# Weight tiles of 128x1024 in rings of three in place of 128x512 in rings of five, and shared places for tiles of the solve and of the samples

## The chip, the cores and the metric

The kernel runs on one core of a Trainium2 chip. The metric is the device time of one execution in microseconds; the kernel before has a median of 2118.79 us in three runs. TensorE is called PE in the profile, VectorE DVE, ScalarE ACT, GpSimd POOL, and SyncE, which issues the DMAs here, SP.

## The reference

One inference step of two layers for a prompt of 272 rows (16 meta tokens and 256 tokens) and 8 samples of one token each; the model width is 2048 and the branch width 4096. All data are fp32.

```python
# layer 0 (mixer A, RWKV-7), for prompt and samples
rkvz = einsum('btpd,pde->btpe', xm[:, :, :4], w_rkvz)        # 4 products 2048 x 4096
...                                                          # decay d, a from two low-rank products; kk normalised per head
S = S * d - (S @ kk) * b + v * k ; y = S @ r                 # 64 heads, state 64 x 64, row after row
y = groupnorm(y) + (r*k*r_k).sum() * v ; o = (y * silu(z)) @ w_out     # 4096 x 2048
# shared keys and values
kv = rmsnorm(h, kv_norm) @ w_kv                              # 2048 x 1024
# layer 1 (mixer B): sliding window of 128, a sink per head, 64 query heads on 8 kv heads
q, z = split(rmsnorm(h, b_norm) @ b_w_qz)                    # 2048 x 8192
h += (attention(q, k, v, sinks) * silu(z)) @ b_w_o           # 4096 x 2048
```

The outputs are the final rows, the RWKV states, the shift rows and the caches of prompt and samples.

## The kernel before

**Weights.** Every weight matrix is read once, in units of 256 KB (`wunits`, L199): 128 partitions by 512 numbers, which are two k-tiles of 256 columns. A unit goes through three engines. SP issues its DMA into `raw` (L211). ACT casts it to `whi`, a rounded fp32r copy (L195, in `split`). DVE subtracts, `wlo = raw - whi` (L197, in `split`). PE then makes three matmuls for each k-tile and half of the columns (`mm3`, L218 to L220: whi by xh, whi by xl, wlo by xh), 12 for a unit, each with 280 moving rows (272 + 8) in layer 0 and 264 in layer 1. There are 1040 such units: 112 named k, 128 each named v, r, z, oa, qb, zb and ob, and 32 named kv. `raw`, `whi` and `wlo` are rings of five tiles each; from the products of out_a on (where `self.wx` is set) every second unit takes its raw tile from another ring of four, `rawx`. A raw tile comes free with its subtract, `whi` and `wlo` with the last matmul that reads them.

**Stages by time.** Phase 0 (to about 155 us) normalises and mixes the inputs. Phase A (to about 1260 us) runs the products r, k, v, z and the first part of the output product, and between their pieces, on the same engines, the recurrence: the preparation of a pair of heads (`prep`), scores, `substitute` and `solve` (a triangular inverse by blocks), `chain` (40 steps of three matmul groups each, with copies on ACT and DVE between), `group_norm` and the samples' `decode`. Then come out_a (to 1376 us), the kv product (to about 1415 us), phase B (attention and the products q and z, to 1912 us) and out_b, with a tail to the end.

**What sets the order.** On PE the order is the program's: `drive` takes a piece of a product (one unit, half of its columns, 6 matmuls) and then whatever a stream has due at that place, so the matmuls of the recurrence stand at fixed places between weight pieces. An engine executes in order, so a small matmul whose operand is late holds the weight matmuls behind it. On DVE, ACT and SP a scheduler sets the order by priority and by `issue_after`; the streams other than the epilogues and the main one are issued after the subtract `self.los[-2]`. `self.raws` and `self.los` hold one entry for each unit, and code elsewhere indexes them by unit.

**Places the change and the prediction touch.** `substitute` (L1053) ends with two transposes on DVE, TN (L1081) and TR (L1082), which `solve` multiplies first (L1102, ps_so). `prep` (L858) loads kT (a ring of two tiles), multiplies it into kk (L898, which waits for a DMA of the key norms that `key_norms` writes), and scans the decays (L910, cl). `group_norm` transposes the result on PE (L1275, ps_yt) and adds it on DVE (L1276, vT), which frees the bank. `decode` multiplies the samples' states into a work tile T, tag dT. In the kv product (from L1490) the casts stand on ACT between operations of `norm_mix` (L1464, bmh).

Of the kernel before, what the change touches and what calls it, by code (L numbers as in the profile page):

```python
# [12 lines left out]
F32 = mybir.dt.float32  # L13
# [96 lines left out]
class Kernel:  # L110
# [10 lines left out]
    def run(self):  # L121
        nc, tc = self.nc, self.tc
        with contextlib.ExitStack() as st:
            pool = lambda n, bufs=1, **k: st.enter_context(tc.tile_pool(name=n, bufs=bufs, **k))
            self.cp = pool("const")
            self.wp = pool("wts", 5)
            self.pm = pool("pm", 3, space=PSUM)
            self.pp = pool("pp", 1, space=PSUM)
            self.pe = pool("pe", 2, space=PSUM)
            self.dp = pool("dram", space=DRAM)  # L130
            self.single_banks()
            self.load_consts()
            self.sp = self.open("stage", bufs=2)
            self.mp = self.open("mix", bufs=8, side="right")
            self.ph = self.open("ph0")
            self.phase0()
            self.close("ph0")
            tile = dict(reuse_waits="tile")

            pools = self.open("late", **tile), self.open("early", **tile)  # L140
            self.rp = Pools(pools, "vT Y ev gmean gvar rsyy rsty")
            self.close("py", "pc")
            self.pcy = self.open("pcy", 1, space=PSUM)
            self.phase_a()
            self.close("pcy")
            self.single_banks()
            self.close("mix")
            right = dict(side="right", **tile)
            self.op = self.open("res", **right)
            self.kvp, self.st0, self.wx0 = (self.open(n, **right) for n in ("kv", "st0", "wx0"))  # L150
            self.out_a()
            self.close("gA", "late", "stage")
            self.bp = self.open("B", **tile)
            self.phase_b()
            self.close("B")
            self.gp = self.open("gB", **tile)
            self.out_b()
            self.wx = None
            self.close("gB", "g1", "st1", "wx1", "g0", "at", "res", "py", "pc")
# [39 lines left out]
    def wunits(self, w, name, nk, col, nc_, per):  # L199

        nc = self.nc
        assert nc_ == 256 and per == 2, (nc_, per)
        for k0 in range(0, nk, per):
            t = lambda n, dt, **k: self.wp.tile([128, 512], dt, tag=n, name=f"{n}_{name}_{col}_{k0}", **k)[
                :, :per * nc_].rearrange("p (k c) -> p k c", k=per)
            if self.wx and len(self.raws) % 2:
                raw = self.wx.tile([128, 512], F32, tag="rawx", bufs=4, name=f"raw_{name}_{col}_{k0}")[
                    :, :per * nc_].rearrange("p (k c) -> p k c", k=per)
            else:
                raw = t("raw", F32, bufs=5)  # L210
            self.raws.append(nc.sync.dma_start(raw.rearrange("p k c -> p (k c)"), w[col // 256, k0 // 2]))  # L211
            hi, lo = t("whi", F32R), t("wlo", F32R)
            self.los.append(self.split(hi, lo, raw))
            yield k0, hi, lo

    def mm3(self, ps, wh, wl, xh, xl, start, stop):
        mm = self.nc.tensor.matmul
# [640 lines left out]
    def prep(self, u):  # L858
        nc, rp, I = self.nc, self.rp, self.I
# [6 lines left out]
        w = lambda n, bufs=1: rp.tile([128, 2, N], F32, tag=n, bufs=bufs, name=f"{n}{u}")  # L866

        raw = rp.tile([LR, 512], F32, tag="lraw", name=f"lraw_{u}")
# [3 lines left out]
        hi = rp.tile([128, 544], F32R, tag="lhi", name=f"lhi_{u}")[:LR, :512]  # L872
        lo = rp.tile([128, 544], F32R, tag="llo", name=f"llo_{u}")[:LR, :512]
# [11 lines left out]
        cl, a = wa  # L885
        if u >= 4:
            yield 0, self.after(6, ('n', u // 4), *(('x', m, p0) for m in range(3)))
        else:
            yield 0, self.after(6, ('x', 0, p0))
        kT = w("kT", 2)  # L890
        dma(kT, self.kd[b][:, sl])
        rT = w("rT")
        dma(rT, self.rd[b][:, sl])
# [44 lines left out]
        g, h0 = p0 // 8, (2 * p0) % 16  # L938
# [114 lines left out]
    def substitute(self, o):  # L1053

        nc, rp = self.nc, self.rp
# [3 lines left out]
        w = lambda n, *s: rp.tile([128, *s], F32, tag=n, name=f"{n}{o}")  # L1059
# [8 lines left out]
        NL = w("NL", 512)  # L1068
        V.transpose(NL, N16.rearrange("p i t -> p t i"))
        nl = NL.rearrange("p (t a s) -> p t a s", a=2, s=16)  # L1070
        for s in range(1, 15):
            n = 15 - s
# [4 lines left out]
            V.tensor_tensor(nl[:, s + 1:16, :, 0:s], nl[:, s + 1:16, :, 0:s], tv, op=AD)  # L1077
        for a in range(2):
            V.memset(NL[:, 16 * a:512:33], 1.0)
        TN, TR = w("TN", 16, 32), w("TR", 16, 32)  # L1080
        V.transpose(TN.rearrange("p s i -> p (s i)"), nl.rearrange("p t a s -> p s a t"))  # L1081
        V.transpose(TR.rearrange("p t i -> p (t i)"), NL)  # L1082
        TT = rp.tile([128, 20, 64], F32, tag="TT", name=f"TT{o}")
# [198 lines left out]
    def decode(self, g):  # L1282
# [18 lines left out]
        NI = 8  # L1301
        rowb = lambda a: a.unsqueeze(1).to_broadcast((128, NI, 64))
        for q in range(64 // NI):
            if q:
                yield 3
            S = rp.tile([128, NI, 64], F32, tag="dS", bufs=1, name=f"dS{g}_{q}")
            T = rp.tile([128, NI, 64], F32, tag="dT", bufs=1, name=f"dT{g}_{q}")
            iq = slice(NI * q, NI * q + NI)
            dma(S.rearrange("p i j -> p (i j)"),
                I['state_wkv'][g, q])  # L1310
            yield 5 if g < 3 else 4, lambda: self.samples
            for w, o in ((kk, sa), (dr, y)):
                tt(T, S, rowb(w), op=MU)
                V.reduce_sum(o[:, iq], T, axis=AX.X)
# [658 lines left out]
```

## Time and profile before

| | |
|---|---|
| three runs | 2116.79, 2118.79 and 2124.86 us, median 2118.79 |
| profiled execution | 2118.32 us, its span 2116.5 us |
| granted PE clock | 0.99 in the mean |
| DMA | 446.28 MB, mean 211 GB/s |
| DVE instructions counted as busy | 4112, 1697.8 us |
| ACT instructions counted as busy | 2790, 1263.8 us |

The span is the stretch from the first to the last recorded event; the profiled execution's time is 1.8 us longer. A row of the waits gives an engine, what it was about to do, what it waited for, the sum of these waits in us, their number and the longest. In rows of the timeline the columns are start, duration, engine, line, operation, tiles (out<-in), and in brackets the idle time before it with its releaser; the lines that the prediction shows are not shown here.

### The profile page before, as it was taken

The page shows a single profiled execution, that of the slowest core. Times are in us where ns is not written, and L with a number is a line of the kernel's source. Part 1 is how long each engine was busy: PE and PEld are TensorE (multiplying, and loading weights), DVE is VectorE, ACT ScalarE, POOL GpSimd, SP SyncE. Part 2 cuts the span into 40 slices and gives each one's busy share as a digit, 9 for nine tenths or more (in the row PEclk, how much of TensorE's full clock was granted, in tenths as well). Part 3 has the DMA queues.
Part 4 walks back from the last instruction along what each step waited for, and adds up shares of the span by engine and source line. Part 5 has one row for each costly group of instructions (what it writes and reads, how often), then busy time and mean ns, then how long its engine had stood idle before and what let it go on. Part 6 is the DMA issues. An engine that isn't in the chain of part 4 may idle for free.

```text
span 2116.5 us, 55871 instructions
## 1 busy us (share of the span) xinstructions
PE 2064.9 (98%) x21420; PEld 1965.8 (93%) x21420; DVE 1697.8 (80%) x4112; ACT 1263.8 (60%) x2790; POOL 122.5 (6%) x188
## 2 busy tenths in 40 slices
PE   9999999899999999999999999999999999999997
PEld 7999899889899989899999999999999999999997
DVE  8867777687678878888888788997888888878885
ACT  3457766576766757767676445565565655544443
POOL 0011100001010010100100001100000000000000
PEclk9999999999999999999999999999999999999999
DMA  7898667658756876777657687757455444567774
GB/s 258 314 312 250 189 213 241 188 181 290 216 180 205 260 229 198 211 217 222 203 152 246 207 257 243 247 172 227 132 167 156 146 155 130 181 210 247 232 219 132
DMA packets 276356, 446.28 MB, mean 211 GB/s; under 512 B 54056, under 2 KB 97768, under 8 KB 275696
## 3 DMA queue, kind: packets, MB, share of 16 engines
q1 hardware_dynamic: 275656, 441.66, 66.6%
q8 instruction: 168, 2.75, 0.5%
q10 hardware_dynamic: 432, 1.05, 0.1%
q14 instruction: 100, 0.82, 0.1%
HBM read 381.69 MB, written 65.03 MB: 211 GB/s over the span
## 4 chain that ended last, share of the span: by engine, by line
PE 87%; DVE 5%; ACT 3%; DMA 3%; issue 2%; SPq 0%; POOL 0%; DVEq 0%; POOLq 0%; ACTq 0%
PE ps_z L218 6%; PE ps_z L219 6%; PE ps_z L220 6%; PE ps_k L218 3%; PE ps_ob L218 3%; PE ps_ob L220 3%; PE ps_v L218 3%; PE ps_ob L219 3%; PE ps_r L218 3%; PE ps_q L218 3%; PE ps_q L220 3%; PE ps_q L219 3%; PE ps_k L219 3%; PE ps_k L220 3%; PE ps_v L220 3%; PE ps_v L219 3%
## 5 line engine op out<-in xcount | busy, mean ns | idle before, releaser
L218 PE MATMUL ps_z<-mhlm,whi_z 128*128 128x280 f32 x512 | 158.6, 310 | 2.8 <-ACT sr L937 2.0
L219 PE MATMUL ps_z<-mhlm,whi_z 128*128 128x280 f32 x512 | 150.6, 294 | 0.0
L220 PE MATMUL ps_z<-mhlm,wlo_z 128*128 128x280 f32 x512 | 150.3, 294 | 0.0
L218 PE MATMUL ps_q<-bmh,whi_qb 128*128 128x264 f32 x512 | 150.0, 293 | 0.1
L218 PE MATMUL ps_z<-bmh,whi_zb 128*128 128x264 f32 x512 | 147.4, 288 | 0.0
L220 PE MATMUL ps_q<-bmh,wlo_qb 128*128 128x264 f32 x512 | 145.6, 284 | 0.6 <-DVE wlo_qb L197 0.6
L219 PE MATMUL ps_q<-bml,whi_qb 128*128 128x264 f32 x512 | 145.6, 284 | 0.0
L219 PE MATMUL ps_z<-bml,whi_zb 128*128 128x264 f32 x512 | 145.5, 284 | 0.0
L220 PE MATMUL ps_z<-bmh,wlo_zb 128*128 128x264 f32 x512 | 145.4, 284 | 0.0
L218 PE MATMUL ps_ob<-ghi,whi_ob 128*128 128x264 f32 x512 | 145.3, 285 | 0.0
L220 PE MATMUL ps_ob<-ghi,wlo_ob 128*128 128x264 f32 x512 | 144.6, 284 | 0.0
L219 PE MATMUL ps_ob<-glo,whi_ob 128*128 128x264 f32 x512 | 144.6, 283 | 0.0
L195 ACT CAST whi_ob<-raw_ob 128x512 fp32r<-128x512 f32 x128 | 79.1, 620 | 96.9 <-PE ps_ob L219 77.8
L195 ACT CAST whi_oa<-raw_oa 128x512 fp32r<-128x512 f32 x128 | 79.2, 620 | 88.0 <-PE ps_oa L219 30.6
L197 DVE TENSOR_TENSOR wlo_r<-raw_r,whi_r 128x512 fp32r<-128x512 f32 x128 | 87.8, 691 | 42.6 <-ACT whi_r L195 41.3
L218 PE MATMUL ps_v<-mhlm,whi_v 128*128 128x280 f32 x384 | 119.8, 312 | 0.4 <-ACT st L790 0.4
L218 PE MATMUL ps_k<-mhlm,whi_k 128*128 128x280 f32 x384 | 119.1, 310 | 1.0 <-ACT st L790 1.0
L195 ACT CAST whi_v<-raw_v 128x512 fp32r<-128x512 f32 x128 | 79.0, 619 | 65.8 <-PE ps_v L219 37.7
L197 DVE TENSOR_TENSOR wlo_v<-raw_v,whi_v 128x512 fp32r<-128x512 f32 x128 | 87.3, 687 | 36.9 <-ACT whi_v L195 35.6
L195 ACT CAST whi_zb<-raw_zb 128x512 fp32r<-128x512 f32 x128 | 78.2, 619 | 62.9 <-PE ps_z L219 38.5
L220 PE MATMUL ps_k<-mhlm,wlo_k 128*128 128x280 f32 x384 | 112.4, 293 | 2.1 <-issue 2.1
L219 PE MATMUL ps_v<-mhlm,whi_v 128*128 128x280 f32 x384 | 112.7, 293 | 0.0
(478 smaller groups left out, 7604.1 us busy)
## 6 DMA issues: line engine op xcount, KB each, us to landing
raw_k<-a_w_rkvz SPq DMA_DIRECT2D x128, 256.0 KB
raw_v<-a_w_rkvz SPq DMA_DIRECT2D x128, 256.0 KB
raw_r<-a_w_rkvz SPq DMA_DIRECT2D x128, 256.0 KB
raw_z<-a_w_rkvz SPq DMA_DIRECT2D x128, 256.0 KB
raw_oa<-a_w_out SPq DMA_DIRECT2D x128, 256.0 KB
raw_qb<-b_w_qz SPq DMA_DIRECT2D x128, 256.0 KB
raw_zb<-b_w_qz SPq DMA_DIRECT2D x128, 256.0 KB
raw_ob<-b_w_o SPq DMA_DIRECT2D x128, 256.0 KB
```

The source lines that it names most:

```text
L195: self.nc.scalar.copy(hi, src)
L197: return self.nc.vector.tensor_tensor(lo, src, hi.bitcast(F32), op=ALU.subtract)
L218: mm(ps, wh, xh, start=start, stop=False)
L219: mm(ps, wh, xl, start=False, stop=False)
L220: return mm(ps, wl, xh, start=False, stop=stop)
```

## The change

`wunits` makes tiles of 128x1024 that hold two consecutive units. One DMA of 512 KB loads both (two runs of 2 KB for each partition), one cast makes both halves of `whi`, one subtract both of `wlo`; `self.raws` and `self.los` get the same entry twice. The three rings have three such tiles, so six units where there were five. From out_a on, every fourth pair takes its raw tile from `rawx`, which has one tile of 128x1024 where it had four of 128x512. The matmuls read halves of the tiles and stay as they are, 12 for a unit.

To make room, three tiles change places: kT has one tile where it had two (so its load for a pair of heads waits for the last reader of the pair before), TN takes a place in the ring `ev` of two, and T of `decode` takes the place of NL, the tile of `substitute`.

```diff
--- before.py
+++ after.py
@@ -123,7 +123,7 @@
         with contextlib.ExitStack() as st:
             pool = lambda n, bufs=1, **k: st.enter_context(tc.tile_pool(name=n, bufs=bufs, **k))
             self.cp = pool("const")
-            self.wp = pool("wts", 5)
+            self.wp = pool("wts", 3)
             self.pm = pool("pm", 3, space=PSUM)
             self.pp = pool("pp", 1, space=PSUM)
             self.pe = pool("pe", 2, space=PSUM)
@@ -199,19 +199,20 @@
     def wunits(self, w, name, nk, col, nc_, per):
 
         nc = self.nc
-        assert nc_ == 256 and per == 2, (nc_, per)
-        for k0 in range(0, nk, per):
-            t = lambda n, dt, **k: self.wp.tile([128, 512], dt, tag=n, name=f"{n}_{name}_{col}_{k0}", **k)[
-                :, :per * nc_].rearrange("p (k c) -> p k c", k=per)
-            if self.wx and len(self.raws) % 2:
-                raw = self.wx.tile([128, 512], F32, tag="rawx", bufs=4, name=f"raw_{name}_{col}_{k0}")[
-                    :, :per * nc_].rearrange("p (k c) -> p k c", k=per)
+        assert nc_ == 256 and per == 2 and nk % 4 == 0, (nc_, per, nk)
+        for k0 in range(0, nk, 4):
+            nm = f"{name}_{col}_{k0}"
+            t = lambda n, dt: self.wp.tile([128, 1024], dt, tag=n, name=f"{n}_{nm}")
+            if self.wx and len(self.raws) // 2 % 4 == 1:
+                raw = self.wx.tile([128, 1024], F32, tag="rawx", bufs=1, name=f"raw_{nm}")
             else:
-                raw = t("raw", F32, bufs=5)
-            self.raws.append(nc.sync.dma_start(raw.rearrange("p k c -> p (k c)"), w[col // 256, k0 // 2]))
+                raw = t("raw", F32)
+            self.raws += [nc.sync.dma_start(raw.rearrange("p (u c) -> p u c", u=2),
+                                            w[col // 256, k0 // 2:k0 // 2 + 2].rearrange("u p c -> p u c"))] * 2
             hi, lo = t("whi", F32R), t("wlo", F32R)
-            self.los.append(self.split(hi, lo, raw))
-            yield k0, hi, lo
+            self.los += [self.split(hi, lo, raw)] * 2
+            for u in range(2):
+                yield k0 + 2 * u, *(a[:, 512 * u:512 * u + 512].rearrange("p (k c) -> p k c", k=per) for a in (hi, lo))
 
     def mm3(self, ps, wh, wl, xh, xl, start, stop):
         mm = self.nc.tensor.matmul
@@ -887,7 +888,7 @@
             yield 0, self.after(6, ('n', u // 4), *(('x', m, p0) for m in range(3)))
         else:
             yield 0, self.after(6, ('x', 0, p0))
-        kT = w("kT", 2)
+        kT = w("kT")
         dma(kT, self.kd[b][:, sl])
         rT = w("rT")
         dma(rT, self.rd[b][:, sl])
@@ -1077,7 +1078,7 @@
             V.tensor_tensor(nl[:, s + 1:16, :, 0:s], nl[:, s + 1:16, :, 0:s], tv, op=AD)
         for a in range(2):
             V.memset(NL[:, 16 * a:512:33], 1.0)
-        TN, TR = w("TN", 16, 32), w("TR", 16, 32)
+        TN, TR = ev("TN", 16, 32), w("TR", 16, 32)
         V.transpose(TN.rearrange("p s i -> p (s i)"), nl.rearrange("p t a s -> p s a t"))
         V.transpose(TR.rearrange("p t i -> p (t i)"), NL)
         TT = rp.tile([128, 20, 64], F32, tag="TT", name=f"TT{o}")
@@ -1304,7 +1305,7 @@
             if q:
                 yield 3
             S = rp.tile([128, NI, 64], F32, tag="dS", bufs=1, name=f"dS{g}_{q}")
-            T = rp.tile([128, NI, 64], F32, tag="dT", bufs=1, name=f"dT{g}_{q}")
+            T = rp.tile([128, 512], F32, tag="NL", name=f"dT{g}_{q}").rearrange("p (i j) -> p i j", i=NI)
             iq = slice(NI * q, NI * q + NI)
             dma(S.rearrange("p i j -> p (i j)"),
                 I['state_wkv'][g, q])
```

Line numbers after `wunits` are higher by one in the changed kernel. Over the whole program the busy instructions on DVE fall by 520, those on ACT by 520, and SP's DMA issues from 1785 to 1265.

The first place is on DVE, ahead of the first solve (about 252 to 256 us): the end of `substitute`, with TN, for which PE waits in ps_so. kk and cl belong to the preparation of a later pair of heads, wlo_r is a weight subtract. Before:

```order
L197 TENSOR_TENSOR wlo_r_10_3533<-raw_r_10_3530,whi_r_10_3532 128x512
L898 SCALAR_TENSOR_TENSOR kk_3641<-kT_3637,par,kk_3641 128x280 x2
L1075 TENSOR_TENSOR stmp_14_3002<-NL_2961 128x28
L910 SCALAR_TENSOR_TENSOR cl_3338<-reset,cl_3338 128x272 x2
L1077 TENSOR_TENSOR NL_2961<-NL_2961,stmp_14_3002 128x2x14
L1081 STREAM_TRANSPOSE TN_3007<-NL_2961 128x512
L1082 STREAM_TRANSPOSE TR_3008<-NL_2961 128x512
```

Now:

```order
L1078 TENSOR_TENSOR NL_2685<-NL_2685,stmp_13_2723 128x4x13
L1076 TENSOR_TENSOR stmp_14_2726<-NL_2685 128x28
L1078 TENSOR_TENSOR NL_2685<-NL_2685,stmp_14_2726 128x2x14
L1082 STREAM_TRANSPOSE TN_2731<-NL_2685 128x512
L1083 STREAM_TRANSPOSE TR_2732<-NL_2685 128x512
L1105 COPY ET_3171<-ps_so_3106 128x256
L197 TENSOR_TENSOR wlo_r_12_3298<-raw_r_12_3295,whi_r_12_3297 128x1024
L899 SCALAR_TENSOR_TENSOR kk_3311<-kT_3307,par,kk_3311 128x280 x2
L911 SCALAR_TENSOR_TENSOR cl_3026<-reset,cl_3026 128x272 x2
```

The products kk and the scans cl, which stood between the last steps of NL and TN, now stand behind TN, TR, the copy ET and a weight subtract.

The second place is on DVE in the product v, at the second solve and the first group norm (about 371 to 382 us); ps_yt is PE's bank of the group norm, which vT frees. kk is the row that waits for the DMA of the key norms. Before:

```order
L898 SCALAR_TENSOR_TENSOR kk_5449<-kT_5445,par,kk_5449 128x280
L1075 TENSOR_TENSOR stmp_14_5118<-NL_5077 128x28
L898 SCALAR_TENSOR_TENSOR kk_5449<-kT_5445,par,kk_5449 128x280
L910 SCALAR_TENSOR_TENSOR cl_4871<-reset,cl_4871 128x272 x2
L904 TENSOR_TENSOR kT_5445<-kT_5445,km_4_5454 128x280
L1077 TENSOR_TENSOR NL_5077<-NL_5077,stmp_14_5118 128x2x14
L197 TENSOR_TENSOR wlo_v_14_5425<-raw_v_14_5422,whi_v_14_5424 128x512
L904 TENSOR_TENSOR kT_5445<-kT_5445,km_4_5457 128x280
L906 TENSOR_TENSOR ta_4872<-ta_4872,kk_5449 128x560
L1081 STREAM_TRANSPOSE TN_5123<-NL_5077 128x512
L1082 STREAM_TRANSPOSE TR_5124<-NL_5077 128x512
L1276 SCALAR_TENSOR_TENSOR vT_2043<-ps_yt_0_5399,par,vT_2043 128x272
```

Now:

```order
L1076 TENSOR_TENSOR stmp_14_4674<-NL_4633 128x28
L1078 TENSOR_TENSOR NL_4633<-NL_4633,stmp_14_4674 128x2x14
L1082 STREAM_TRANSPOSE TN_4679<-NL_4633 128x512
L1083 STREAM_TRANSPOSE TR_4680<-NL_4633 128x512
L197 TENSOR_TENSOR wlo_v_12_4933<-raw_v_12_4930,whi_v_12_4932 128x1024
L911 SCALAR_TENSOR_TENSOR cl_4445<-reset,cl_4445 128x272 x2
L899 SCALAR_TENSOR_TENSOR kk_4969<-kT_4965,par,kk_4969 128x280 x2
L1277 SCALAR_TENSOR_TENSOR vT_1857<-ps_yt_0_4925,par,vT_1857 128x272
L905 TENSOR_TENSOR kT_4965<-kT_4965,km_4_4974 128x280
```

TN, TR and the weight subtract now stand ahead of kk, so do the scans cl, and the products kT stand behind vT; between kk and vT no other row is left.

## The prediction

> **What bounds the kernel now.** I read the page first, then the stretches of 200 us, the waits of PE, ACT and SP, and last the timeline around the longest waits. The page:
>
> ```profile
> span 2116.5 us, 55871 instructions
> PE 2064.9 (98%) x21420; PEld 1965.8 (93%) x21420; DVE 1697.8 (80%) x4112; ACT 1263.8 (60%) x2790; POOL 122.5 (6%) x188
> PE 87%; DVE 5%; ACT 3%; DMA 3%; issue 2%; SPq 0%; POOL 0%; DVEq 0%; POOLq 0%; ACTq 0%
> ```
>
> PE is busy for 98% of the span. It stands for 2116.5 - 2064.9 = 51.6 us, and the change leaves all of its matmuls as they are. So the time can fall by the part of the 51.6 us that DVE and ACT cause, and by what follows such waits; it can rise without a bound of that kind. The stretches show where PE stands (columns: span, busy us and count of PE, PEld, DVE, ACT, POOL, granted clock, DMA share, GB/s):
>
> ```profile
> 200.00:400.00 200.00, 188.22 (x2357) 176.44 (x2356) 144.32 (x331) 130.23 (x287) 18.69 (x28) 0.97 0.67 211
> 600.00:800.00 200.00, 195.41 (x2578) 183.34 (x2578) 162.52 (x358) 130.48 (x282) 18.09 (x28) 0.98 0.71 223
> 1600.00:1800.00 200.00, 200.00 (x1719) 192.40 (x1717) 167.52 (x632) 116.05 (x320) 0.00 (x0) 1.00 0.49 147
> 1800.00:2000.00 200.00, 200.00 (x1657) 199.26 (x1656) 166.00 (x309) 100.90 (x177) 5.30 (x6) 1.00 0.70 217
> ```
>
> In phase B and out_b PE never stands, though DVE is 84% busy there; in phase A it loses 11.8 us in one stretch and 4.6 in another. The waits of PE say for whom:
>
> ```profile
> PE ps_yt L1275 <- DVE vT L1276: 8.0, 2, 6.9
> PE ps_so L1102 <- DVE TN L1081: 6.1, 2, 3.5
> PE ps_z L218 <- ACT sr L937: 2.0, 1, 2.0
> PE ps_kv L218 <- ACT whi_kv L195: 1.8, 1, 1.8
> PE ps_ch L1205 <- ACT W L1196: 1.3, 2, 0.9
> PE ps_ch L1191 <- DVE X L1227: 1.1, 1, 1.1
> PE ps_ch L1214 <- ACT X L1210: 1.1, 2, 0.9
> PE ps_q L220 <- DVE wlo_qb L197: 0.6, 2, 0.4
> ```
>
> Weights are waited for in two rows only, 1.8 + 0.6 = 2.4 us in 1040 units. The large waits are for the recurrence: 14.1 us in the first two rows. The stream of weights is ahead, as the waits of ACT and of SP's queue show:
>
> ```profile
> ACT whi_ob L195 <- PE ps_ob L219: 77.8, 55, 1.9
> ```
> ```profile
> SPq L211 <- DVE wlo_zb L197: 110.0, 85, 8.3
> ```
>
> The cast waits for PE to free a place, the DMA for a subtract to free one. A faster cast or transfer by itself therefore buys nothing. What can matter is where a cast or a subtract stands ahead of an operand of the recurrence.
>
> A wait costs more than its length. Behind the 6.9 us wait, in two adjoining stretches:
>
> ```profile
> 383.00:388.00 5.00, 5.00 (x27) 4.99 (x26) 1.66 (x5) 2.82 (x5) 0.00 (x0) 0.58 0.66 210
> 388.00:398.00 10.00, 10.00 (x316) 9.57 (x315) 6.49 (x14) 4.98 (x13) 0.32 (x1) 1.00 0.66 196
> ```
> ```profile
> 386.16 0.43 PE L218 MATMUL ps_v<-mhlm,whi_v 128*128 128x280 f32 x1
> 386.40 0.43 PE L219 MATMUL ps_v<-mhlm,whi_v 128*128 128x280 f32 x1
> ...
> 388.12 0.29 PE L218 MATMUL ps_v<-mhlm,whi_v 128*128 128x280 f32 x1
> 388.25 0.29 PE L219 MATMUL ps_v<-mhlm,whi_v 128*128 128x280 f32 x1
> ```
>
> The granted clock is 0.58 in the first stretch and 1.00 in the second; matmuls of 280 rows start 0.24 us apart in the one and 0.13 in the other. Counted over the trace by such start times, there are seven stretches of 3 to 5 us at half clock, each behind a wait, and they cost 11.6 us in all.
>
> **The change part by part.** The prices:
>
> ```profile
> L195 ACT CAST whi_z<-raw_z 128x512 fp32r<-128x512 f32 x128 | 78.3, 617 | 37.4 <-PE ps_z L219 25.4 <-DMA raw_z<-a_w_rkvz 4.0 <-DVE wlo_z L197 2.5
> L195 ACT CAST ghi<-at 128x1056 fp32r<-128x1056 f32 x8 | 8.4, 1069 | 0.0
> ```
> ```profile
> L197 DVE TENSOR_TENSOR wlo_zb<-raw_zb,whi_zb 128x512 fp32r<-128x512 f32 x128 | 86.3, 688 | 26.0 <-ACT whi_zb L195 19.0 <-PE ps_z L219 5.1 <-PE ps_q L219 1.3
> L197 DVE TENSOR_TENSOR glo<-at,ghi 128x1056 fp32r<-128x1056 f32 x8 | 9.8, 1252 | 0.0
> ```
> ```profile
> 41.39 3.09 DVE L197 TENSOR_TENSOR wlo_k<-raw_k,whi_k 128x512 fp32r<-128x512 f32 x5
> ```
>
> *Work.* From 512 to 1056 columns the cast grows by 0.452 us and the subtract by 0.564, so at 1024 they take about 0.617 + 0.425 = 1.04 and 0.688 + 0.531 = 1.22 us. A pair took 1.23 and 1.38 apart, or, back to back, 2 x 3.09/5 = 1.24 on DVE. So a subtract saves 0.02 to 0.16 us of a pair, 8 to 83 us of DVE over 520 pairs, and a cast up to 0.19 us, 99 us of ACT. None of it is on PE, and where PE is at 100% it is worth nothing. I count it only where a late operand waits behind weights. The Trainium skill ("Perfetto Trace Analysis", section "Optimizing Scalar/DVE Operations") says that grouping improves throughput if the engine is saturated. No stretch shows DVE above 84%, so by that rule the 1.0 us that the chain gains below would be nothing, and the sum 1.0 us higher.
>
> *Latency.* The first half of a pair is ready after 1.04 + 1.22 = 2.26 us where a unit took 1.31: 0.95 us later. The cover is the ring. A pair is 24 matmuls of 0.13 us, 3.1 us on PE. Where a pair is used half by half (phase B, out_a, out_b), a place of five came free 1.5 pairs ahead of the next use, 4.7 - 1.3 = 3.4 us of lead; of three pairs, 2 pairs ahead, 6.2 - 2.3 = 3.9 us. In phase A, with units freed one by one, five gave 4 units, 6.2 - 1.3 = 4.9 us, and pairs, freed with their second half, give 6.2 - 2.3 = 3.9. The lead shrinks by 1 us in phase A and grows by half a microsecond elsewhere, and stays above nothing. I put the cost at nothing; if the cover went, 0.95 us at each of the 520 pairs would be the bound.
>
> *DMA.* 520 transfers of 512 KB for 1040 of 256 KB, the same bytes; SP issues 520 fewer. A place is asked for again three pairs ahead (9.3 us) where it was five units (7.8 us); at 211 GB/s a pair takes 2.5 us and a unit 1.2 us, so the slack is 6.8 against 6.6 us. A small DMA that stands behind a pair waits up to 1.3 us more; the key norms at the second place below are such.
>
> *The first place.*
>
> ```profile
> 252.75 0.92 DVE L898 SCALAR_TENSOR_TENSOR kk<-kT,par,kk 128x280 f32<-128x280 f32 x2
> 253.69 1.33 DVE L910 TENSOR_TENSOR_SCAN cl<-reset,cl 128x272 f32<-128x272 f32 x2
> 255.14 1.05 DVE L1081 STREAM_TRANSPOSE TN<-NL 128x512 f32<-128x512 f32 x1
> ```
> ```profile
> 256.24 1.27 PE L1102 MATMUL ps_so<-TN,Noff 32*32 32x16 f32 x128 [3.50 <-DVE TN L1081]
> ```
>
> kk and cl, 0.92 + 1.33 = 2.25 us, leave the path to TN. The single subtract ahead of them becomes half of a pair that stands earlier, about 0.3 us more. The wait goes from 3.5 to about 1.0 us: -2.5. Behind it lay 1.6 us of the half clock's 11.6; after a wait of 1 us half of that may stay: -0.8. What is late next is ET, the copy behind TN and TR; nothing new stands before it.
>
> *The second place.*
>
> ```profile
> 375.65 0.51 DVE L898 SCALAR_TENSOR_TENSOR kk<-kT,par,kk 128x280 f32<-128x280 f32 x1 [4.24 <-DMA kk<-kr]
> ...
> 381.45 0.46 DVE L1276 SCALAR_TENSOR_TENSOR vT<-ps_yt,par,vT 128x272 f32<-128x272 f32 x1
> ```
> ```profile
> 381.96 0.90 PE L1275 MATMUL ps_yt<-consts,Y 128*128 128x128 f32 x3 [6.92 <-DVE vT L1276]
> ```
>
> DVE stands at kk for the DMA, and from the landing (375.65) to PE's start 381.96 - 375.65 = 6.3 us pass. In the new order only kk (0.92) and vT (0.46) are behind the landing, 1.4 us: 4.9 less. The landing comes later by what the chain of key norms waits behind pairs: 0 to 2 us on DVE and in the queue, I take 1. That leaves 6.9 - 4.9 + 1 = 3.0 us: -3.9. The half clock behind it (2.0 us of the 11.6) stays.
>
> *The rest.* The other wait for TN (6.1 - 3.5 = 2.6 us, at 913 us) loses a small subtract of 0.35 and some savings: -0.7. The chain's and ET's waits lose tenths each: -1.0. At the kv product a longer cast and subtract follow the operations for which PE waits 1.8 us: +0.5. kT with one place: its load waits for the last reader of the pair before, as rT and kk with their single places do already: 0, at most what one more wait for a load costs, 1 to 2 us. T in NL's place: both are on DVE alone, in order: 0. New lateness from operands behind a longer cast or subtract (+0.42 or +0.53 us each, at a few places): +1.0 in the range 0 to 6.
>
> The sum is -2.5 - 0.8 - 3.9 - 0.7 - 1.0 + 0.5 + 1.0 = -7.4 us, against the profiled 2118.3 (span and 1.8 us around it; the median, 2118.8, lies 0.5 above): 2118.3 - 7.4 = **2110.9**. With the savings of the two places between half and all of their waits and clock (3.5 + 1.6 + 6.9 + 2.0 = 14 us), and the last term at its ends, this case reaches from 2102 to 2119.
>
> **The rivals.** *The loosened DVE pays all along* (faster). The savings per pair accumulate wherever DVE has a queue, and most waits on DVE and ACT go: 14.1 + 2.0 + 1.3 + 1.1 + 1.1 us of the rows above, some 3 us of smaller ones, and the 11.6 us of half clock, 34 us in all; two thirds to all of it gives 2084 to 2096, and half, 2101. For it: DVE is 72 to 84% busy. Against: at most places PE waits for a chain of several steps, not for a weight op.
>
> *The moves cancel* (no change). The scheduler sets another order at every pair, so waits end at one place and arise at another: 2116 to 2122. For it: TN is late at two of the eight solves alone, which shows that it is chance what stands ahead.
>
> *Longer operations hold the chain* (slower). The place is `chain`, whose steps wait for copies that stand in order behind casts and subtracts:
>
> ```profile
> L1196 ACT COPY W<-ps_ch x32: 352/373/377, 279.5 to 1217.9; 128x256 f32<-128x256 f32 x32
> ```
>
> PE waited for W, X and FS copies five times (3.5 us), of 40 steps with three groups of matmuls each, 120 waits. A copy that comes while a cast runs waits up to 0.42 us longer, behind a subtract 0.53. If a third of the 120 are late by 0.5 us, that is 40 x 0.5 = 20 us, and some of them bring half clock of 1.5 us, 4 such: 6 us. Less the 7 us of the two places: 2118 + 26 - 7 = 2137. It decides as soon as the slack of these groups lies below 0.5 us at more than about 25 of them. For it: ACT's casts come once each 1.55 us of PE. Against: only five of 120 are late now, by at most 1.1 us, and ACT is 60% busy, less in the new kernel. The Trainium skill has the rule for this rival in the section named above ("Perfetto Trace Analysis", "Optimizing Scalar/DVE Operations"): "If Scalar/Vector aren't saturated, but are causing bubbles on other engines, breaking up instructions may allow work to be completed sooner." By it the change goes the wrong way, since the rows show DVE at 80% and bubbles on PE; by the order, the two largest bubbles come from what stands ahead of TN and vT and not from an operation's length.
>
> **How the numbers follow.** The forecast gets 0.55, the full gain 0.18, the cancelling 0.14, the slower case 0.13. Faster by over 0.5% (about what a measurement of this kernel can tell from no change) is below 2108.2: 0.22 of the forecast's 0.55 and all of the full gain, 0.40. Slower by over 0.5% is above 2129.4: 0.12. The same is 0.48. The range runs from 2093, which leaves out some 0.1 of the full gain, to 2127, which leaves out some 0.1 of the slower case.
>
> **What would show it.** Right: the wait of ps_so for TN near 256 us is about 1 us, that of ps_yt near 382 us about 3 us, with DVE standing at kk and only kk and vT behind the landing; 1024-wide casts take 1.04 us and subtracts 1.22; weight waits of PE stay under 5 us; phase B and out_b keep PE at 200 of 200 us. Wrong: waits of PE for wlo or whi in phase B or phase A of more than 10 us, chain waits (L1191, L1205, L1214) above 10 us, or a landing of kk that is later by over 3 us.

## The result and the profile after

The changed kernel takes 2131.91 us (median of 7 runs, 2127.93 to 2135.44), the kernel before 2120.59 (7 runs, 2116.79 to 2124.86). The ratio is 1.0051 with an interval of 1.0036 to 1.0067: slower by about 11 us, where 7 us less was forecast. The profiled execution took 2135.44 us, the longest of the seven. The ratio given below for the run with raw by pairs leaves out one of its executions that took 8491 us, four times the others.

The page of the changed kernel:

```profile
span 2133.6 us, 52847 instructions
PE 2070.5 (97%) x21420; PEld 1971.0 (92%) x21420; DVE 1655.8 (78%) x3592; ACT 1181.7 (55%) x2270; POOL 120.0 (6%) x188
PE 82%; DVE 7%; DMA 4%; issue 3%; ACT 3%; SPq 1%; POOL 0%; DVEq 0%; POOLq 0%; ACTq 0%
```

DVE lost 42 us of work and ACT 82 us, and still PE stands longer: 2133.6 - 2070.5 = 63.1 us where it was 51.6. The other 5.6 us are in PE's own busy time. Up to the tail, the trace's record of the granted clock has ten stretches at 0.50 in place of seven. PE works through 39.0 us of them in place of 28.5; at half speed 5.2 us of that are lost time, nearly all of the 5.6. The stretches of the prediction, with the same columns:

```profile
200.00:400.00 200.00, 194.53 (x2469) 182.85 (x2468) 146.58 (x294) 126.73 (x249) 17.81 (x29) 0.98 0.67 216
600.00:800.00 200.00, 190.31 (x2508) 178.10 (x2507) 158.22 (x310) 123.74 (x237) 15.24 (x28) 0.99 0.69 221
1600.00:1800.00 200.00, 200.00 (x1719) 192.56 (x1719) 161.79 (x591) 107.92 (x268) 0.00 (x0) 1.00 0.45 147
1800.00:2000.00 200.00, 200.00 (x1663) 198.49 (x1663) 158.83 (x266) 90.59 (x127) 4.64 (x4) 1.00 0.64 212
```

From 200 to 400 us PE gains 6.3 us of work, about as forecast (the terms of the two places came to 7.2). Phase B and out_b are as full as before. The loss lies between, here as two long stretches of the kernel before and of the changed one:

```profile
600.00:1290.00 690.00, 674.58 (x8516) 636.99 (x8516) 572.75 (x1288) 448.97 (x976) 46.83 (x74) 0.99 0.69 216
1290.00:1500.00 210.00, 207.65 (x1634) 204.74 (x1634) 181.99 (x420) 116.92 (x252) 17.67 (x20) 0.99 0.70 214
```
```profile
600.00:1290.00 690.00, 658.67 (x8300) 620.43 (x8299) 548.09 (x1112) 418.45 (x806) 43.90 (x74) 0.98 0.65 209
1290.00:1500.00 210.00, 204.38 (x1593) 202.03 (x1592) 171.50 (x326) 100.41 (x169) 19.65 (x20) 0.98 0.67 215
```

In the later part of phase A PE stands 15.9 us longer, around the kv product and the start of phase B 3.3 us longer (the kv product's last matmul ends at 1432 us in the kernel before, not at about 1415, and at 1449 in the changed one). The waits of PE in the changed kernel:

```profile
PE ps_yt L1276 <- DVE vT L1277: 4.7, 3, 2.3
PE ps_so L1103 <- DVE TN L1082: 4.2, 2, 2.2
PE ps_so L1109 <- issue: 4.0, 3, 3.2
PE ps_ch L1192 <- ACT X L1228: 3.8, 4, 2.3
PE ps_z L219 <- ACT st L791: 3.6, 2, 3.4
PE ps_dy L1338 <- DVE dy L1335: 2.5, 1, 2.5
PE ps_kv L221 <- DVE wlo_kv L197: 2.1, 1, 2.1
PE ps_kv L219 <- ACT whi_kv L195: 1.6, 1, 1.6
```

The two rows that were to shrink did: 8.0 + 6.1 us became 4.7 + 4.2. Below them stand many new ones of 2 to 4 us, for copies and small results on ACT and DVE, and 4.0 us for which the trace gives no releaser ("issue"); for weights PE waits at the kv product alone.

### The profile page after: what moved, and what is told of

Its sections match the earlier page's. It is cut to its first block, busy times and chain, and to the rows that moved or that the text cites. A ratio compares the mean times of both kernels' runs of the same rounds, so it can differ in the third digit from the quotient of the medians.

```text
span 2133.6 us, 52847 instructions
## 1 busy us (share of the span) xinstructions
PE 2070.5 (97%) x21420; PEld 1971.0 (92%) x21420; DVE 1655.8 (78%) x3592; ACT 1181.7 (55%) x2270; POOL 120.0 (6%) x188
## 3 DMA queue, kind: packets, MB, share of 16 engines
q8 instruction: 168, 2.75, 0.5%
q10 hardware_dynamic: 432, 1.05, 0.1%
## 4 chain that ended last, share of the span: by engine, by line
PE 82%; DVE 7%; DMA 4%; issue 3%; ACT 3%; SPq 1%; POOL 0%; DVEq 0%; POOLq 0%; ACTq 0%
PE ps_z L219 5%; PE ps_z L220 5%; PE ps_z L221 5%; PE ps_v L219 3%; PE ps_k L219 3%; PE ps_ob L219 3%; PE ps_ob L221 3%; PE ps_ob L220 3%; PE ps_q L219 3%; PE ps_v L220 3%; PE ps_q L220 3%; PE ps_v L221 3%; PE ps_q L221 3%; PE ps_k L220 3%; PE ps_k L221 3%
## 5 line engine op out<-in xcount | busy, mean ns | idle before, releaser
L195 ACT CAST whi_ob<-raw_ob 128x1024 fp32r<-128x1024 f32 x64 | 67.3, 1051 | 114.4 <-PE ps_ob L220 72.0
L219 PE MATMUL ps_k<-mhlm,whi_k 128*128 128x280 f32 x384 | 119.2, 310 | 2.9 <-issue 1.8
L195 ACT CAST whi_oa<-raw_oa 128x1024 fp32r<-128x1024 f32 x64 | 67.2, 1050 | 92.2 <-PE ps_oa L220 34.8
L220 PE MATMUL ps_k<-mhlm,whi_k 128*128 128x280 f32 x384 | 112.8, 294 | 0.7 <-issue 0.7
L221 PE MATMUL ps_v<-mhlm,wlo_v 128*128 128x280 f32 x384 | 112.2, 292 | 0.0
L197 DVE TENSOR_TENSOR wlo_v<-raw_v,whi_v 128x1024 fp32r<-128x1024 f32 x64 | 78.7, 1229 | 42.3 <-ACT whi_v L195 39.1
L197 DVE TENSOR_TENSOR wlo_r<-raw_r,whi_r 128x1024 fp32r<-128x1024 f32 x64 | 78.1, 1221 | 42.5 <-ACT whi_r L195 36.4
```

The lines of the kernel that those rows point to most:

```text
L195: self.nc.scalar.copy(hi, src)
L197: return self.nc.vector.tensor_tensor(lo, src, hi.bitcast(F32), op=ALU.subtract)
L219: mm(ps, wh, xh, start=start, stop=False)
L220: mm(ps, wh, xl, start=False, stop=False)
L221: return mm(ps, wl, xh, start=False, stop=stop)
```

## The experiments

After the result I held theory 1: longer casts and subtracts, and casts that wait for the place of a whole pair (1b), stand in order ahead of operands of the recurrence. The rivals: the shared places (2), the landing of a 512 KB transfer (3), the streams issued after the subtract of a later unit, since `self.los` now holds each pair's twice (4), and later, issue two by two by itself (5). Every time is a median, every ratio goes against runs of the kernel before on the same chip (medians 2117.4 to 2119.2 us).

**The shared places alone.** The kernel before with

```diff
-        kT = w("kT", 2)
+        kT = w("kT")
-        TN, TR = w("TN", 16, 32), w("TR", 16, 32)
+        TN, TR = ev("TN", 16, 32), w("TR", 16, 32)
-            T = rp.tile([128, NI, 64], F32, tag="dT", bufs=1, name=f"dT{g}_{q}")
+            T = rp.tile([128, 512], F32, tag="NL", name=f"dT{g}_{q}").rearrange("p (i j) -> p i j", i=NI)
```

> The kernel before with its rings of five tiles of 128x512, one DMA, cast and subtract for each unit, and only the three shared places of the change (kT one tile, TN in the ring ev, T of decode in the place of NL). Theory 1 (longer casts and subtracts, and casts that wait for a whole pair, stand in order ahead of the recurrence's operands): 2115 to 2123 us, as the kernel before. Rival 2 (the shared places make loads or DVE work of the recurrence late): 2128 to 2136, as the changed kernel. Rival 3 (transfers of 512 KB land late): as the kernel before. Rival 4 (the streams are issued after the subtract of a later unit): as the kernel before.

Measured: 2120.49 us, ratio 1.0006 (0.9994 to 1.0018). Rival 2 falls. The order of casts and subtracts among the other operations of ACT and DVE is the same as before.

**Six single tiles.** The same, and

```diff
-            self.wp = pool("wts", 5)
+            self.wp = pool("wts", 6)
-            if self.wx and len(self.raws) % 2:
-                raw = self.wx.tile([128, 512], F32, tag="rawx", bufs=4, name=f"raw_{name}_{col}_{k0}")[
+            if self.wx and len(self.raws) // 2 % 4 == 1:
+                raw = self.wx.tile([128, 512], F32, tag="rawx", bufs=2, name=f"raw_{name}_{col}_{k0}")[
-                raw = t("raw", F32, bufs=5)
+                raw = t("raw", F32)
```

> The shared places, and the place that they free used for rings of six tiles of 128x512 in place of five; every unit has its own DMA, cast and subtract. The weights get as many places as in the changed kernel, but singly. Theory 1: 2112 to 2122 us, no slower than the kernel before. Rival 2: 2128 to 2136. Rival 3: as theory 1. Rival 4: as theory 1.

Measured: 2118.92 us, 1.0009 (0.9998 to 1.0019). The room of the changed kernel, used singly, costs nothing and brings nothing.

**Pairs of tiles, operations by halves.** The changed kernel with

```diff
-            self.los += [self.split(hi, lo, raw)] * 2
+            for s in (slice(0, 512), slice(512, 1024)):
+                self.los.append(self.split(hi[:, s], lo[:, s], raw[:, s]))
```

> The changed kernel with its double tiles, its rings of three and its DMAs of 512 KB, but with two casts and two subtracts of 128x512 for a pair, both issued where the one stood. Places still come free by pairs. Theory 1 in its form that the length of an operation does it: 2117 to 2124 us; in its form that the wait of the pair's first cast for a place does it: 2128 to 2136. Rival 2: 2128 to 2136. Rival 3: 2128 to 2136. Rival 4: 2117 to 2134, since the streams are issued after the first half's subtract, one unit earlier.

Measured: 2134.36 us, 1.0085 (1.0069 to 1.01). The length of an operation is not the cause: with the old lengths, though not with the old places, the loss is all there. Theory 1 is left with 1b.

**Two DMAs of 256 KB.** The changed kernel with

```diff
-            self.raws += [nc.sync.dma_start(raw.rearrange("p (u c) -> p u c", u=2),
-                                            w[col // 256, k0 // 2:k0 // 2 + 2].rearrange("u p c -> p u c"))] * 2
+            self.raws += [nc.sync.dma_start(raw[:, 512 * u:512 * u + 512], w[col // 256, k0 // 2 + u]) for u in range(2)]
```

> The changed kernel with two DMAs of 256 KB for each pair in place of one of 512 KB; casts and subtracts stay 128x1024. Theory 1: 2128 to 2136 us, as the changed kernel. Rival 2: the same. Rival 3 (the landing of a whole pair): 2117 to 2124. Rival 4: 2128 to 2136.

Measured: 2132.78 us, 1.0068 (1.0053 to 1.0082). Rival 3 falls.

**Six single tiles, issued two by two.** `wunits` makes both units' tiles, DMAs, casts and subtracts before it yields the first.

```diff
-            yield k0, hi, lo
+                two.append((k0, hi, lo))
+            yield from two
```

> Rings of six tiles of 128x512 and the shared places, as in the second run, but the DMA, cast and subtract of two consecutive units are issued together, one after the other, as the changed kernel does with its pairs; places still come free one by one. Theory 1b (a place comes free only when PE has read the whole pair, and the cast that waits for it holds what stands behind it on ACT and DVE): 2114 to 2123 us, as the run with single issue. Theory 5 (issuing by pairs puts the second unit's cast and subtract earlier, ahead of operations of the recurrence): 2127 to 2137, as the changed kernel.

Measured: 2121.16 us, 1.0012 (1.0002 to 1.0022). The middle of the interval is about a quarter of the loss and its upper end less than half; theory 5 falls as the main cause.

**The hook, and pairs asked for later.** Two edits of the changed kernel:

```diff
-                        turn = self.tc.issue_after(self.los[-2].ins) if self.pos and s[0] not in now else \
+                        turn = self.tc.issue_after(self.los[-3].ins) if self.pos and s[0] not in now else \
```

> The changed kernel with the streams issued after the subtract of the pair before the last in place of the last pair's (self.los[-3] for self.los[-2]). Rival 4 (the streams' operations stand too late because the list now holds each pair's subtract twice): 2114 to 2124 us. Theory 1b: 2127 to 2137, as the changed kernel, since the casts wait for the same places. Theory 5: in between or as the changed kernel.

```diff
-                while len(W) <= h or sum(k >= h - 1 for k in range(len(W))) < 4 and not over:
+                while len(W) <= h or sum(k >= h - 1 for k in range(len(W))) < 3 and not over:
```

> The changed kernel with its pairs asked for one unit later in phase A (three units held ahead in place of four), so that a pair's DMA, cast and subtract are issued half a pair later in the program's order. Theory 5: 2116 to 2125 us, most of phase A's loss gone. Theory 1b: half or more of the loss gone in phase A, 2118 to 2128, since a cast issued later finds its place free or nearly so. Rival 4: 2127 to 2137 or slower, since the hook stays. If the weights lack the lead, slower than 2137, with waits of PE for wlo.

Measured: 2127.57 us, 1.004 (1.0021 to 1.0059), and 2127.79, 1.005 (1.0034 to 1.0066). The first lies at the lower edge of what theory 1b expected and outside what rival 4 did; the second lies inside both, at the upper edge of 1b, and outside what theory 5 expected. Against the changed kernel's 1.0051 (1.0036 to 1.0067) neither is a difference clear of noise, so neither order gives the loss back. Rival 4 falls by a run below as well: with whi alone by pairs `self.los` holds a subtract of its own for each unit, and the loss is there.

**Raw by pairs, or whi and wlo by pairs.** With six single tiles for the rest: first raw as three tiles of 128x1024 with one DMA, then whi and wlo as three tiles of 128x1024 each; casts and subtracts by halves in both.

```diff
-                    raw = t("raw", F32)
+                raw = self.wp.tile([128, 1024], F32, tag="raw", bufs=3, name=f"raw_{nm}")
```

> Shared places; raw tiles by pairs of 128x1024 in a ring of three with one DMA of 512 KB, but whi and wlo as six single tiles of 128x512 with a cast and a subtract each, issued two by two. Theory 1b in the form that it is whi and wlo, whose places PE frees: 2116 to 2124 us. In the form that it is raw, whose places the subtracts free: 2127 to 2137. Theory 5: 2119 to 2123, as the run with issue two by two.

```diff
-                hi, lo = t("whi", F32R), t("wlo", F32R)
+            hi, lo = (self.wp.tile([128, 1024], F32R, tag=n, bufs=3, name=f"{n}_{nm}") for n in ("whi", "wlo"))
```

> Shared places; raw as six single tiles with a DMA of 256 KB each, but whi and wlo as tiles of 128x1024 in rings of three, each written by two casts or subtracts of 128x512 and read by halves. Theory 1b in the form that it is whi and wlo: 2128 to 2137 us, as the changed kernel; in the form that it is raw: 2116 to 2124.

Measured: 2122.23 us, 1.0018 (1.0 to 1.0036), and 2131.91, 1.0075 (1.0056 to 1.0093). The cost is in the tiles that PE reads.

**Four single places.** The run with six single tiles, and

```diff
-            hi, lo = t("whi", F32R), t("wlo", F32R)
+            hi, lo = t("whi", F32R, bufs=4), t("wlo", F32R, bufs=4)
```

> The run with six single tiles, but whi and wlo in rings of four (raw stays six). If it is the number of places that PE has left ahead (four units, as many as lie between the use of a pair and the release of its place): 2126 to 2140 us. If it is that a place opens only every 3.1 us, by pairs, while single places open every 1.55 us: 2116 to 2126, since single places open as often as before.

Measured: 2134.7 us, 1.009 (1.0075 to 1.0105). By the time alone this would say that it is the number of places. The waits of PE say otherwise:

```profile
PE ps_q L220 <- DVE wlo_qb L197: 4.6, 10, 0.9
...
PE ps_z L220 <- DVE wlo_zb L197: 3.3, 8, 0.5
```

With four places PE waits for weights in phase B and out_b, 10.1 us after 1500 us; in the changed kernel it does not, and with whi and wlo by pairs it does not either. Between 160 and 1290 us the waits of PE come to 30.8 us; in the kernel before they are 33.3, in the changed one 42.5, with whi and wlo by pairs 48.4. So it is another loss at another place.

**Whi alone, wlo alone.** Six single tiles for the rest, casts and subtracts by halves, issued two by two (for wlo alone the test below is `n == "wlo"`):

```diff
-                hi, lo = t("whi", F32R), t("wlo", F32R)
+            his, los, two = halves("whi"), halves("wlo"), []
...
+                if n == "whi":
+                    a = self.wp.tile([128, 1024], F32R, tag=n, bufs=3, name=f"{n}_{nm}")
+                    return a[:, :512], a[:, 512:]
+                return [self.wp.tile([128, 512], F32R, tag=n, name=f"{n}_{nm}_{u}") for u in range(2)]
```

> Shared places, raw as six single tiles; whi as tiles of 128x1024 in a ring of three, wlo as six single tiles; casts and subtracts of 128x512, issued two by two. If the damage comes from the cast that waits on ACT for a pair's place: 2126 to 2136 us. If it comes from the subtract that waits on DVE for a pair's place: 2117 to 2123. If either is enough, or both add up: about 2125.

> The opposite: wlo as tiles of 128x1024 in a ring of three, whi and raw as six single tiles. If the damage comes from the cast on ACT: 2117 to 2123 us; if from the subtract on DVE: 2126 to 2136; if either is enough or both add up: about 2125.

Measured: whi by pairs 2131.7 us, 1.0066 (1.0051 to 1.0081); wlo by pairs 2120.41, 1.001 (1.0 to 1.0021). The run issued two by two (1.0012) is the control for both, and both at once gave 1.0075. The whole loss comes with whi, whose place the cast on ACT waits for. The waits of ACT for it in the product z, between 160 and 1270 us, in four kernels: before, changed, whi by pairs, wlo by pairs (sum, times, longest).

```profile
ACT whi_z L195 <- PE ps_z L219: 25.4, 31, 2.2
```
```profile
ACT whi_z L195 <- PE ps_z L220: 31.3, 22, 3.6
```
```profile
ACT whi_z L195 <- PE ps_z L224: 21.0, 20, 3.2
```
```profile
ACT whi_z L195 <- PE ps_z L224: 30.8, 39, 2.2
```

In z, with single places, ACT stands often and shortly, 0.8 us in the mean; with pairs a half to two thirds as often, but 1.05 to 1.4 us, and up to 3.6. Over all products of these 1110 us the means are 0.86 us before and 1.33 in the changed kernel, but the sum falls, from 130.5 us in 151 waits to 112.1 in 84, and the longest do not separate the kernels: 3.2 and 6.3 us, and 8.8 with six single tiles issued two by two, which cost next to nothing. With wlo by pairs DVE's subtracts stand 43.2 us for PE (38 times, up to 3.6 us) where it was 2.0 us, once, in the kernel before, in part instead of standing for the cast (48.9 us where it was 125.2), and that costs next to nothing.

The kv product shows what such a wait does, at a place that repeats to a hundredth of a microsecond from run to run. On ACT a block of 13 operations `bmh` of `norm_mix` (14 with whi by pairs) with two table loads stands behind the eighth unit's cast, and the ninth cast behind the block. With wlo by pairs (whi single) on ACT, and PE's waits:

```profile
1383.93 0.62 ACT L195 CAST whi_kv<-raw_kv 128x512 fp32r<-128x512 f32 x1 [0.66 <-ACT sqa L1450]
1384.70 0.62 ACT L195 CAST whi_kv<-raw_kv 128x512 fp32r<-128x512 f32 x1 [0.15 <-PE ps_kv L224]
1385.34 1.28 ACT L1461 ACT_TABLE_LOAD   x1
...
1394.50 1.12 ACT L195 CAST whi_kv<-raw_kv 128x512 fp32r<-128x512 f32 x2
```
```profile
1381.49 0.29 PE L223 MATMUL ps_kv<-kvh,whi_kv 128*128 128x280 f32 x1
...
1395.16 0.39 PE L223 MATMUL ps_kv<-kvh,whi_kv 128*128 128x280 f32 x1 [0.22 <-ACT whi_kv L195]
1396.82 0.40 PE L225 MATMUL ps_kv<-kvh,wlo_kv 128*128 128x280 f32 x1 [0.49 <-DVE wlo_kv L197]
```

With whi by pairs:

```profile
1398.29 1.14 ACT L195 CAST whi_kv<-raw_kv 128x512 fp32r<-128x512 f32 x2 [1.58 <-issue]
1399.45 1.28 ACT L1461 ACT_TABLE_LOAD   x1
...
1408.78 1.12 ACT L195 CAST whi_kv<-raw_kv 128x512 fp32r<-128x512 f32 x2
```
```profile
1394.70 0.29 PE L223 MATMUL ps_kv<-kvh,whi_kv 128*128 128x280 f32 x1
...
1409.43 0.40 PE L223 MATMUL ps_kv<-kvh,whi_kv 128*128 128x280 f32 x1 [1.29 <-ACT whi_kv L195]
1412.18 0.40 PE L225 MATMUL ps_kv<-kvh,wlo_kv 128*128 128x280 f32 x1 [1.98 <-DVE wlo_kv L197]
```

Counted from the first matmul of the product, the table load starts at 3.85 us with single places and at 4.75 with pairs; the next cast follows at 13.0 and 14.1, with one more operation of 0.42 us ahead of it. With single places the eighth unit's cast starts at 3.2 us, when its place comes free, and the seventh is done by then. With pairs both start at 3.6 (1398.29), behind the 24 matmuls of the first pair, the last of which ends at 3.25; for the rest the trace gives no releaser, but raw and wlo are single in both kernels and the cast moves with whi alone. PE pays 1.29 + 1.98 in place of 0.22 + 0.49. The changed kernel shows it with the same 13 operations in the block:

```profile
1394.78 1.28 ACT L1457 ACT_TABLE_LOAD   x1
...
1403.68 1.03 ACT L195 CAST whi_kv<-raw_kv 128x1024 fp32r<-128x1024 f32 x1
```

Its first matmul is at 1389.74, so its table load is at 5.04 us and its next cast at 13.94, 0.93 later than with single places; PE's waits are the 1.6 and 2.1 in its rows further above. In the kernel before ACT's times are those of the single places, 3.85 and 13.0, but with five places it is the seventh unit's cast that stands ahead of the block; PE, which needs the eighth after 84 matmuls and not the ninth after 96, waits 1.77 us.

**Four pairs of whi.** With raw in four single tiles to make room, and the control for that:

```diff
-                    a = self.wp.tile([128, 1024], F32R, tag=n, bufs=3, name=f"{n}_{nm}")
+                    a = self.wp.tile([128, 1024], F32R, tag=n, bufs=4, name=f"{n}_{nm}")
-                    raw = self.wp.tile([128, 512], F32, tag="raw", name=f"raw_{nm}_{u}")
+                    raw = self.wp.tile([128, 512], F32, tag="raw", bufs=4, name=f"raw_{nm}_{u}")
```

> As the run with whi alone in pairs, but with four pairs of whi in place of three (the room comes from raw, four single tiles in place of six); wlo six single tiles, casts and subtracts of 128x512. If three pairs are one place too few: 2117 to 2123 us. If it is that two places of whi open at once, whatever their number: 2126 to 2136.

> The control for it: whi and wlo six single tiles, issued two by two, raw four single tiles in place of six. If four raw tiles cost nothing: 2117 to 2123 us, as with six; if they starve the casts: 2125 or more, and the other run has to be read against this one.

Measured: 2159.61 us, 1.0191 (1.0167 to 1.0215); the control 2138.41, 1.0092 (1.0078 to 1.0106). The control already loses with four raw tiles, so whether three pairs of whi are too few stays open. The first of the two shows ACT's queue from another side. Its casts stand earlier in ACT's order, by 2.3 units in the mean against the kernel before, and wait there for transfers; PE then waits for the chain's copies behind them, and most of all for TN on DVE (12.3 us in two waits). Its waits of ACT and of PE:

```profile
ACT whi_r L195 <- DMA raw_r<-a_w_rkvz: 47.6, 34, 5.8
```
```profile
PE ps_ch L1210 <- ACT W L1201: 6.0, 4, 2.9
PE ps_ch L1219 <- ACT X L1215: 4.7, 4, 2.4
```

**The second place by itself.** The kernel before with

```diff
-            yield 0, self.after(6, ('n', u // 4), *(('x', m, p0) for m in range(3)))
+            yield 0, self.after(12, ('n', u // 4), *(('x', m, p0) for m in range(3)))
```

> The kernel before with one number changed: the preparation of the later pairs of heads starts its loads 12 pieces of a product after the key norms in place of 6, so that on DVE kk and cl stand behind the group norm's first two vT near 382 us. It tests the term of the second place by itself, without pairs. If that wait (6.9 us and 2.0 us of half clock) goes and nothing becomes late in its place: 2108 to 2113 us. If the order of DVE there gives it back elsewhere: 2115 to 2121.

Measured: 2112.91 us, 0.9974 (0.9963 to 0.9984): the fastest of all, 5 us below the kernel before on the same chip. The row of the group norm's wait in it:

```profile
PE ps_yt L1275 <- DVE vT L1276: 3.5, 4, 1.2
```

8.0 us with a longest of 6.9 became 3.5 with a longest of 1.2. Other rows rose: all of PE's waits after 160 us are 34.7 us where they were 35.9, the chain's 6.4 where they were 3.7. The profiled execution (2117.64) is the slowest of the twelve, so how much of the 5 us this one wait gives is not shown.

## Why the prediction was wrong

**The bound** was read rightly: PE is full in phase B and out_b, weights do not reach PE late in phase A, and the time went by waits for the recurrence.

**Prices.** Right: casts of 1024 columns took 1.05 us (1.04 forecast), subtracts 1.23 (1.22). In the changed kernel's groups:

```profile
L195 ACT CAST whi_v<-raw_v 128x1024 fp32r<-128x1024 f32 x64 | 67.0, 1047 | 51.2 <-PE ps_v L220 28.7 <-PE ps_k L220 12.6 <-issue 7.7
L197 DVE TENSOR_TENSOR wlo_v<-raw_v,whi_v 128x1024 fp32r<-128x1024 f32 x64 | 78.7, 1229 | 42.3 <-ACT whi_v L195 39.1 <-PE ps_ch L1218 2.7 <-DMA rT<-rd 0.2
```

**The second place.** Right. DVE, and PE behind it, in the changed kernel:

```profile
374.33 0.93 DVE L899 SCALAR_TENSOR_TENSOR kk<-kT,par,kk 128x280 f32<-128x280 f32 x2 [1.43 <-DMA kk<-kr]
375.18 0.50 DVE L1277 SCALAR_TENSOR_TENSOR vT<-ps_yt,par,vT 128x272 f32<-128x272 f32 x1
```
```profile
375.73 0.88 PE L1276 MATMUL ps_yt<-consts,Y 128*128 128x128 f32 x3 [2.29 <-DVE vT L1277]
```

Only kk and vT are behind the landing, 1.4 us, and PE waits 2.3 us (3.0 forecast, 6.9 before). The landing, at 374.33 in place of 375.65, is 0.3 us later against PE's arrival, where 1 was assumed. The run that moves only this preparation gives 5 us in all.

**The first place.** Half right: kk and cl left the path, but the wait is 2.2 us and not 1.0.

```profile
252.64 1.23 DVE L197 TENSOR_TENSOR wlo_r<-raw_r,whi_r 128x1024 fp32r<-128x1024 f32 x1 [1.11 <-ACT whi_r L195]
...
254.71 1.04 DVE L1082 STREAM_TRANSPOSE TN<-NL 128x512 f32<-128x512 f32 x1
```
```profile
255.80 1.65 PE L1103 MATMUL ps_so<-TN,Noff 32*32 32x16 f32 x128 [2.24 <-DVE TN L1082]
```

I had the subtract "half of a pair that stands earlier"; it stands there with a wait of 1.11 us for its cast, which itself stood 0.93 us for its transfer, and 1.23 us of its own. The 0.8 us for the half clock behind did not come: a stretch of 3.4 us stands there before and after. (By the trace's record of the clock, the seven stretches of the kernel before cost 14.3 us and not 11.6. And the busiest stretch of 200 us had DVE at 87%, from 1200 to 1400 us, not at 84%.) The third term, the other wait for TN, came as forecast: 4.2 - 2.2 = 2.0 us (2.6 - 0.7).

**The step that failed** is the latency paragraph, which put the cost of pairs at nothing, and the term that came of it, "+1.0 in the range 0 to 6" for late operands. I compared the leads of the weights at PE (3.9 against 3.4 or 4.9 us) and found them above nothing. The leads did hold: PE waits for no weight in phase A. But the waits of PE after 160 us rose from 35.9 to 48.1 us, although the three terms gave 1.3 + 4.6 + 0.6 = 6.5 back, so 18.7 us are new. Of these 5.1 are in rows with "issue" (8.9 us where it was 3.8), which are no operands; about 13.6 us are late operands, where 1.0 was forecast, and three more stretches at half clock came with the waits. The chain's waits, which were to fall by tenths, rose from 3.7 to 8.4, and those for weights at the kv product, with +0.5 forecast, from 1.8 to 3.7. In the place of "nothing" the runs show that places of whi which come free by pairs cost 0.4 to 0.9%, while PE still finds its weights in time. A lead at PE does not tell how long a cast stands for its place at the head of ACT's queue, with the recurrence behind it; I did not cost that, and at the kv product it can be seen. None of the three signs of being wrong came true (waits for weights 3.7 us, for the chain 8.4, the landing of kk 0.3 us later).

**The rivals.** The slower one had the sign and, by luck, about the size (2137 against 2132) with the wrong mechanism. It put it on the length of casts and subtracts, which the run by halves excludes, and saw the chain's copies alone, which brought 4.7 us of the new waits. The quoted rule of the Trainium skill ("Perfetto Trace Analysis", section "Optimizing Scalar/DVE Operations") warned of the right sign; but breaking the instructions up again gave nothing back as long as the tiles stayed double. "The moves cancel" is not it either: kernels with five or six single whi tiles and as many places for raw differ in order on ACT by up to a unit in the mean, and with the old place of kk they keep to 2117.4 to 2122.2 us; all with whi by pairs are above 2127.

**What stays open.** That whi by pairs brings the loss is shown by the runs; that a pair's cast makes what stands behind it on ACT late is shown at the kv product, which is 1.9 us of the new waits. That the 16 us of phase A come by the same way is not shown, and the traces do not bear it out. I followed each wait of PE between 160 and 1290 us back for 6 us, from releaser to releaser. The waits that lead over a cast of whi which had stood for PE come to 7.6 us before, 6.6 in the changed kernel, 7.5 with whi by pairs, 5.9 with six single tiles issued two by two and 0.0 with wlo by pairs; followed for 20 us, they are 7.6, 7.5, 13.8, 10.6 and 2.2. Neither set of sums goes with the times of all five. The order on ACT shifts too (by half a unit in the mean between the runs with whi and with wlo by pairs), and no run separates the shift from the wait. By lead alone it can't be: the first cast of a pair waits for what a ring of five waits for, the second for what a ring of six does, and both rings cost nothing. Each of these traces is one execution, for whi by pairs the slowest of six.

## What to carry to other kernels

A ring's place has two prices: how late its data reach the consumer, and what the order of the engine that fills it makes late. Doubling a tile kept the first here, and with whi it still cost up to 0.9%. Which ring stands it was not to be foretold: raw (2122.23 us) and wlo (2120.41) could be doubled and whi (2131.7) not, though PE frees wlo as it does whi, and DVE has work of the recurrence behind as ACT has. So try each ring by itself. And a wait for a distant DMA in an engine's order (kk here) is cheap to move: moving it gave 5 us, when all the work saved gave nothing.

## What the hardware showed beside that

ACT lost 82 us of busy time and DVE 42 without any gain, in a kernel where PE is 97% busy. And PE stands within a group of 128 small matmuls of the solve with no releaser in the trace (the row of L1109 with "issue" above), between 767 and 801 us in all 17 traces of this case: 1.7 us before, 3.2 in the changed kernel, 4.0 with wlo by pairs. The trace's packets suggest for what. The page lists a queue of kind "instruction", q8, with 168 packets and 2.75 MB, all of 16 KB. Each of the 67 waits of PE above 0.5 us that have no releaser, in the 17 traces, ends 1.2 to 1.7 us after such a packet; these come 12.6 us apart in the mean. In the kernel before PE goes on at 781.39, 1.41 us behind one. So PE most likely stands there for its own instructions; no run tested it, and the sum of these waits (3.8 us before, 8.6 in the changed kernel) differs between kernels of about equal time (3.9 with six single tiles, 9.5 with wlo by pairs).
